# Block sums of the up weights made by accumulating transfers

## The chip, the cores and the metric

The kernel runs on one core of a Trainium2 chip. A core has a matrix engine (TensorE, PE in the profile, with its weight loads as PEld), a vector engine (VectorE, DVE), a scalar engine (ScalarE, ACT), GpSimd (POOL), a queue processor that issues transfers (SyncE, SP) and 16 DMA engines that all transfers share. The engines run side by side and wait for one another by semaphores; each works through its own instructions in order. The metric is the device time of one execution in microseconds.

## The reference

One layer of a diffusion backbone over 1024 tokens of width 1024. A token mixer with two kinds of attention is followed by a layer norm and a ConvFFN, which is the part that matters here:

```python
def _conv_ffn(h, w_up, conv_w, conv_b, w_down):
    u = h @ w_up                                # (1024 x 1024) @ (1024 x 5632)
    half = CONV_WIDTH // 2                      # width 3, one filter per channel
    u = lax.conv_general_dilated(u, conv_w[:, None, :], window_strides=(1,), padding=((half, half),),
                                 dimension_numbers=("NWC", "WIO", "NWC"),
                                 feature_group_count=u.shape[-1]) + conv_b
    gate, val = jnp.split(u, 2, axis=-1)
    return (jax.nn.silu(gate) * val) @ w_down
...
        x = _layer_norm(DEEPNORM_ALPHA * x + gate1 * y, ln1_g[l], ln1_b[l])
        h = x * (1.0 + scale2) + shift2
        y = _conv_ffn(h, w_up[l], conv_w[l], conv_b[l], w_down[l])
```

All numbers are fp32. `w_up` has 22 blocks of 128 gate columns and 22 of 128 value columns.

## The kernel before

**Precision.** An fp32 matrix is split into a high part (rounded to the matrix engine's format, on ACT) and a low part (the rest: a subtraction on DVE or GpSimd). A product then takes three matmuls, high x high, high x low, low x high (`split`, `mm3`). So every weight tile costs a cast and a subtraction before PE can use it.

**Stages.** Attention runs to about 765 us, then the branch merge, the output projection and the first layer norm to about 960 us, the up stage to 1363 us, the down stage and the second layer norm to the end.

**The up stage.** Tiles j = 0, 1, 2 are computed plainly (`up_conv`). Tiles 3 to 21 (`up_tile`) use a Strassen-Winograd scheme with seven products in place of eight. The 2 x 2 blocks on the weights' side are: A11, A12 the gate columns of tile j for the lower and upper half of the 1024 input channels, A21, A22 the value columns likewise. The activations' blocks B11, B21, B12, B22 are the two halves of the channels by the two halves of the tokens. Sums of blocks are needed on both sides:

- weights, per tile: S1 = A21 + A22, S2 = S1 - A11, S3 = A11 - A21, S4 = A12 - S2 (`wsums`, four additions of 128 x 512 on GpSimd into the tiles s12 and s34);
- activations, once: T1 to T4 in the tiles t13 and t24 (`build`, four steps k, each split into T13h, T13l, T24h, T24l).

Each product is 4 x 3 = 12 matmuls of 512 columns, so a tile is 84 matmuls. They accumulate in four PSUM banks a, b, c, d, and the results are combined on the way out: `pe` and `ve` are scratch tiles, `ug` and `uv` the gate and value rows before the convolution, `tg` and `tv` after it. The convolution of one half is an ACT activation and two DVE steps (`conv3`), then Silu on ACT, a product on DVE (`gated`) and a store of 512 KB to DRAM (`gd`).

**Loads and splits.** `wload(j)` loads the gate and value blocks of a tile as two transfers of 512 KB into a ring of three buffers (`raw`, tiles ru0 and ru1). `pairs` splits a weight or a sum into a tile of one of two rings (`w` and `wd`, four buffers each); the high parts are cast on ACT, and the table `UE` says which engine makes the low part: DVE for five of the seven, GpSimd for S4 and A22. The sums live in a ring of four buffers, `m`, which `build` uses for t13 and t24 before it. Three of the value rows' additions out of PSUM are on DVE and one is on GpSimd (the last argument of `add`).

**What sets the order.** PE's order is that of the code (a manual schedule). On ACT, DVE, GpSimd and SP a scheduler orders the instructions when the kernel is built. In the steady state it casts and splits the weights of tile j + 1 during tile j.

The convolution's weights lie in `cvw` and are loaded near the end of attention, when `cvt`, the tile they share with attention's row statistics, comes free.

Of the kernel before, what the change touches and what calls it, by code (L numbers as in the profile page):

```python
# [22 lines left out]
NF = FF // P  # L23
# [4 lines left out]
HALF = 512  # L28
# [24 lines left out]
OTB = 2  # L53
PSU = 6, 7, 2, 3, 4, 5, 0, 1
PSO = 4, 5, 0, 1, 7, 6, 2, 3
UE = "vector", "vector", "vector", "vector", "vector", "gpsimd", "gpsimd"
LN2_P = 1, 2, 2
GAP = 1
LN1_S = slice(0, 512), slice(512, 768), slice(768, 1024)
# [6 lines left out]
def layer_kernel(  # L66
# [6 lines left out]
    nc = tc.nc  # L73
    PSUM = bass.MemoryType.PSUM

    def split(src, hi, lo, hi_eng, lo_eng):
        if hi_eng is nc.scalar:
            nc.scalar.copy(hi, src)  # L78
# [4 lines left out]
        lo_eng.tensor_tensor(out=lo, in0=src, in1=hi.bitcast(F32), op=ALU.subtract)  # L83
# [24 lines left out]
    cvw, cvb = cvt[:, 0:6 * NF].rearrange("p (a b) -> p a b", b=3), cvt[:, 6 * NF:8 * NF]  # L108
# [115 lines left out]
    for k in range(KT):  # L224
# [5 lines left out]
        for t in range(NT):  # L230
            s = slice(t * P, (t + 1) * P)
# [437 lines left out]
    for n, (gi, k) in enumerate(order):  # L669
# [160 lines left out]
    av_issue(True)  # L830
    nc.sync.dma_start(cvw, conv)
# [208 lines left out]
    def sub(e, o, a, b, op=ALU.subtract):  # L1040
        e.tensor_tensor(out=o, in0=a, in1=b, op=op)
# [30 lines left out]
    def build(k):  # L1072
        (b11, b21), (b12, b22) = [[z[:, a] for a in (0, 1)] for z in (zt_[k, 0], tp["v", k])]
        st = {}

        def parts(a, e):
            for p in "hl":
                tp[a + p, k] = ht(f"T{a}{p}_{k}", (P, 2, HALF), R32)
            nc.scalar.copy(tp[a + "h", k], st[a])
            sub(e, tp[a + "l", k], st[a], tp[a + "h", k].bitcast(F32))  # L1080

        def s1():
            st["13"] = t = tm(f"t13_{k}").rearrange("p (a q) -> p a q", a=2)
            sub(nc.vector, t[:, 1], b12, b11)
            sub(nc.gpsimd, t[:, 0], b22, b12)

        def s2():
            st["24"] = t = tm(f"t24_{k}").rearrange("p (a q) -> p a q", a=2)
            sub(nc.vector, t[:, 1], b22, st["13"][:, 1])
            sub(nc.gpsimd if k % 2 else nc.vector, t[:, 0], b21, t[:, 1])  # L1090
            hput(f"z{k}_0", f"v{k}")

        return [s1, s2, lambda: parts("13", nc.vector), lambda: parts("24", nc.vector)]
# [158 lines left out]
        ps3.tile([P, HALF], F32, tag=f"u{n}", name=f"u{n}")  # L1252

    def wload(j):
        wraw[j] = [post.tile([P, 8, P], F32, tag="raw", name=f"ru{gv}_{j}", bufs=3) for gv in (0, 1)]
        for gv in (0, 1):
            nc.sync.dma_start(wraw[j][gv], w_up[2 * j + gv])
        (a11, a12), (_, a22) = [[r[:, 4 * n:4 * n + 4].rearrange("p a b -> p (a b)") for n in (0, 1)]
                                for r in wraw[j]]
        wsrc[j, "A11"], wsrc[j, "A12"], wsrc[j, "A22"] = a11, a12, a22  # L1260

    def wsums(j, mk):
        (a11, a12), (a21, a22) = [[r[:, 4 * n:4 * n + 4].rearrange("p a b -> p (a b)") for n in (0, 1)]
                                  for r in wraw.pop(j)]
# [4 lines left out]
        wsrc.update({(j, "S1"): s12[:, 0], (j, "S2"): s12[:, 1], (j, "S3"): s34[:, 0], (j, "S4"): s34[:, 1]})  # L1269
# [17 lines left out]
    def add(o, p, q, e=nc.vector):  # L1287
        e.tensor_tensor(out=o, in0=p, in1=q, op=ALU.add)  # L1288

    lohalf, hihalf = slice(0, HALF), slice(HALF, T)  # L1290

    def up_tile(j):
        a, b, c, d = (bank(f"{n}{j}") for n in "abcd")
        pe, ve = ht(f"pe{j}", (P, 2, HALF)), ht(f"ve{j}", (P, 2, HALF))
        ug, uv, tg, tv = (ht(f"{n}{j}") for n in ("ug", "uv", "tg", "tv"))
        prod(j, "A11", a, True, True)
        nc.scalar.copy(pe[:, 0], a)
# [9 lines left out]
        nc.scalar.copy(pe[:, 1], c)  # L1307
# [5 lines left out]
        add(ug[:, hihalf], c, ve[:, 0])  # L1313
        conv3(tg, ug, j)
        nc.scalar.activation(tg, tg, AF.Silu)
        pairs(j + 1, "S2", "S3", "S1")
        prod(j, "A22", d, False, True)
        add(uv[:, lohalf], d, ve[:, 0])
        conv3(tv, uv, NF + j)
        gated(j, tg, tv)  # L1320
        hput(*[f"{n}{j}" for n in ("pe", "ug", "ve", "uv", "tg", "tv")])

    wload(NCL)
    wsums(NCL, tm)
# [46 lines left out]
    for j in range(NF):  # L1371
        w, g = wdl.pop(0)
# [221 lines left out]
```

## Time and profile before

| | us |
|---|---|
| median of 3 runs | 1631.38 (1628.08 to 1635.48) |
| the profiled execution | 1630.69 |
| its span, on which all times below stand | 1628.9 |
| tiles 3 to 21 of the up stage | 994.7 to 1363.6 |

In a row of a timeline stand the start, the duration, the engine, the line, the operation, output and inputs by the program's names (without numbers), the shape, the count, and in square brackets the time that the engine stood idle before and what it waited for. In a group of instructions stand the shape and count, then busy time and the mean of one in ns, then the idle time before them and its causes. In a table by windows stand, for each stretch, the busy time of each engine with its count, the granted clock of PE, the mean busy share of the DMA engines and what they moved. `s` in the profile stands for s12 and s34, `wA` for the split weights and `wS` for the split sums, `t` for t13 and t24, `ru` for ru0 and ru1. SPq is SP's queue.

### The profile page before, as it was taken

Reading aid. Unit: us, or ns where it says so; the run is one execution under the profiler, and the core shown is the slowest. Engines: PE = TensorE matmul, PEld = TensorE weight load, DVE = VectorE, ACT = ScalarE, POOL = GpSimd, SP = SyncE. Lnnn points to the kernel's source line nnn. Section 1 sums busy time; section 2 is a strip of 40 time slices with the busy share of each in tenths; the row PEclk is TensorE's granted clock in tenths of the full one; section 3 lists DMA queues with packets and bytes.
Section 4 is the critical chain, followed back from the end, with each engine's and each line's share of the span. In section 5 each row is a group of like instructions: output and inputs, shape, how many; then the busy total and the mean of one; then the engine's idle time right before and its main releaser. Section 6 shows DMA issues by size and latency. Waiting matters only on the chain.

```text
span 1628.9 us, 22394 instructions
## 1 busy us (share of the span) xinstructions
PE 1563.2 (96%) x7944; PEld 1303.5 (80%) x7944; DVE 1173.0 (72%) x1692; ACT 813.5 (50%) x1468; POOL 844.0 (52%) x756
## 2 busy tenths in 40 slices
PE   6999999999999999999999989999999999999996
PEld 5878788888877887777788877888888888888896
DVE  7797646548887677887756695899999996335445
ACT  5322222358887667777223563444444444443343
POOL 0573302526665555655225353666776663337785
PEclk9999999999999999999999999999999999999998
DMA  9695662322230111011440211222222228653453
GB/s 379 211 318 179 213 206 84 117 74 60 61 100 21 46 33 46 24 27 61 158 155 32 99 65 65 78 78 78 78 80 89 88 97 301 218 189 96 149 164 110
DMA packets 86801, 192.52 MB, mean 118 GB/s; under 512 B 11040, under 2 KB 25888, under 8 KB 86688
## 3 DMA queue, kind: packets, MB, share of 16 engines
q1 hardware_dynamic: 81648, 181.63, 33.7%
q10 hardware_dynamic: 5040, 9.46, 1.6%
q8 instruction: 62, 1.02, 0.2%
q14 instruction: 51, 0.42, 0.1%
HBM read 154.28 MB, written 28.38 MB: 112 GB/s over the span
## 4 chain that ended last, share of the span: by engine, by line
PE 80%; DVE 7%; ACT 4%; DMA 3%; issue 3%; POOL 2%; SPq 0%; ACTq 0%; DVEq 0%; POOLq 0%
PE ptr L524 5%; PE g L86 3%; PE g L87 3%; PE g L88 3%; PE b L88 3%; PE b L87 3%; PE b L86 3%; PE ya L88 2%; PE ya L87 2%; PE ya L86 2%; PE av L545 2%; PE av L546 2%; PE d L86 2%; PE d L87 2%; PE yl L86 2%
## 5 line engine op out<-in xcount | busy, mean ns | idle before, releaser
L534 DVE TENSOR_TENSOR ptl<-ptr,pth 128x512 fp32r<-128x512 f32 x188 | 125.0, 685 | 22.5 <-ACT pth L533 19.8
L533 ACT CAST pth<-ptr 128x512 fp32r<-128x512 f32 x188 | 106.7, 587 | 63.7 <-PE ptr L524 37.6
L524 PE MATMUL ptr<-ident,p 128*128 128x128 f32 x816 | 127.2, 278 | 7.0 <-DVE ptl L534 5.1
L420 ACT ACTIVATE p<-p,nm 128x1024 f32<-128x1024 f32 (+2 forms) x128 | 125.3, 981 | 5.6 <-DVE p L453 4.6
L524 PEld LDWEIGHTS ptr<-ident,p 128*128 128x128 f32 x816 | 94.0, 140 | 36.7 <-DVE ptl L534 13.1
L545 PE MATMUL av<-pth,VT 128*128 128x512 f32 x236 | 104.4, 442 | 0.7 <-ACT avs L551 0.5
L83 POOL TENSOR_TENSOR wlg<-wg,whg 128x512 fp32r<-128x512 f32 x32 | 44.8, 1407 | 112.9 <-ACT whg L78 112.9
L86 PE MATMUL g<-hh,whg 128*128 128x512 f32 x256 | 99.9, 390 | 0.0
L88 PE MATMUL g<-hh,wlg 128*128 128x512 f32 x256 | 99.7, 390 | 0.0
L87 PE MATMUL g<-hl,whg 128*128 128x512 f32 x256 | 99.6, 389 | 0.0
L546 PE MATMUL av<-ptl,VT 128*128 128x512 f32 x236 | 97.6, 414 | 2.0 <-POOL ptl L83 1.8
L453 DVE TENSOR_SCALAR_CACHE_REDUCE p<-s,cvt,nmc 128x1024 f32<-128x1024 f32 x64 | 84.3, 1339 | 13.4 <-PE s L409 13.2
L83 POOL TENSOR_TENSOR lwf<-rwf,hwf 128x1024 fp32r<-128x1024 f32 (+1 forms) x36 | 82.3, 2302 | 12.4 <-ACT hwf L78 12.4
L86 PE MATMUL yl<-gr,hwf 128*128 128x256 f32 (+1 forms) x264 | 85.4, 323 | 0.0
L88 PE MATMUL yl<-gr,lwf 128*128 128x256 f32 (+1 forms) x264 | 84.2, 319 | 0.1
L87 PE MATMUL yl<-gr,hwf 128*128 128x256 f32 (+1 forms) x264 | 84.0, 318 | 0.0
L408 PE MATMUL s<-KL,q 128*128 128x512 f32 (+2 forms) x192 | 76.1, 396 | 5.1 <-ACT p_x L420 4.3
L83 POOL TENSOR_TENSOR lwd<-rwd,hwd 128x1024 fp32r<-128x1024 f32 x16 | 38.8, 2423 | 75.0 <-ACT hwd L78 60.6
L80 POOL TENSOR_SCALAR pth<-prw 128x512 fp32r<-128x512 f32 x48 | 30.1, 628 | 90.3 <-ACT prw L530 64.8
L182 DVE CUSTOM_DVE_ANT_0 wml<-wml,sc,bmc 128x1024 f32<-128x1024 f32 x32 | 44.6, 1406 | 40.1 <-DMA wml<-in_wmodT_dram 39.8
L409 PE MATMUL s<-KL,q 128*128 128x512 f32 (+2 forms) x192 | 71.5, 373 | 0.0
L1288 POOL TENSOR_TENSOR uv<-ve,pe 128x512 f32<-128x512 f32 x19 | 29.9, 1573 | 77.2 <-DVE ve L1288 38.1
(387 smaller groups left out, 5295.3 us busy)
## 6 DMA issues: line engine op xcount, KB each, us to landing
wml<-in_wmodT_dram SPq DMA_DIRECT2D x48, 512.0 KB
ru<-in_w_up_dram SPq DMA_DIRECT2D x38, 512.0 KB
rwf<-in_w_dnf_dram SPq DMA_DIRECT2D x24, 512.0 KB
rg<-gd SPq DMA_DIRECT2D x44, 256.0 KB
rwd<-in_w_dn_dram SPq DMA_DIRECT2D x22, 512.0 KB
gd<-tg SPq DMA_DIRECT2D x19, 512.0 KB
wm<-in_wmodT_dram SPq DMA_DIRECT2D x16, 512.0 KB
wg<-in_w_g_dram SPq DMA_DIRECT2D x32, 256.0 KB
```

What stands on the lines that cost most here:

```text
L83: lo_eng.tensor_tensor(out=lo, in0=src, in1=hi.bitcast(F32), op=ALU.subtract)
L86: nc.tensor.matmul(ps, a[0], b[0], start=start, stop=False, skip_group_check=resumed)
L87: nc.tensor.matmul(ps, a[0], b[1], start=False, stop=False, skip_group_check=resumed)
L88: nc.tensor.matmul(ps, a[1], b[0], start=False, stop=stop, skip_group_check=resumed)
L408: nc.tensor.matmul(o, self.q[0][:, hs], ks, start=True, stop=False)
L420: nc.scalar.activation(p, s, AF.Exp, bias=nm[:, h:h + 1], scale=scale, accum_out=sm[:, h:h + 1])
L453: nc.vector.tensor_scalar(out=p, in0=o, scalar1=self.qscale(nqs)[:, hs] if self.br else -1.0, scalar2=self.other[:, hs], op0=ALU.mult, op1 ...
L524: nc.tensor.transpose(tr[:, h * P:(h + 1) * P], self.pslice(h, n), ident)
L533: nc.scalar.copy(hi, tr)
L534: nc.vector.tensor_tensor(out=lo, in0=tr, in1=hi.bitcast(F32), op=ALU.subtract)
L545: nc.tensor.matmul(self.av, v, hi, start=first, stop=False)
L546: nc.tensor.matmul(self.av, v, lo, start=False, stop=self.left == 0)
```

## The change

1. The sums of the weights' blocks are no longer computed on GpSimd. `wsums` makes two tiles, s32 (S3 and S2) and s41 (S4 and S1). SP loads A21 into both halves of both; then GpSimd issues five transfers that add to what lies there: A11 to both halves of s32 (512 KB), A22 to both halves of s41 (512 KB), A22 to S2 (256 KB), A11 to S4 and A12 to S4 (256 KB each). An addition to bytes that an earlier transfer writes waits for it.
2. An accumulating transfer only adds. So the value rows of the scheme are computed with the sign turned: the subtractions of `build` change their order, S2's product is subtracted from `pe`, and the convolution's weights of the value columns of tiles 3 to 21 are multiplied by -1 once, by a new DVE instruction behind their load.
3. `wload` loads only the upper half of the value block (A22, 256 KB).
4. The low parts of S4 and A22 and the fifth addition of the value rows go from GpSimd to DVE. GpSimd has no vector work left in these tiles.
5. S1's product changes places with S3's; it is added straight from PSUM into `uv`, so one copy out of PSUM on ACT (128 x 512) is gone. `pe` and `ve` become the halves of one tile, `pv`.

GpSimd's instructions for one tile in the middle of the stage, before:

```order
L1041 TENSOR_TENSOR s12_9_11238<-ru1_9_11235 128x512
L1041 TENSOR_TENSOR s34_9_11239<-ru0_9_11234,ru1_9_11235 128x512
L1041 TENSOR_TENSOR s12_9_11238<-s12_9_11238,ru0_9_11234 128x512
L83 TENSOR_TENSOR wA22_8_11231<-ru1_8_11093,wA22_8_11231 128x512
L1041 TENSOR_TENSOR s34_9_11239<-ru0_9_11234,s12_9_11238 128x512
L1288 TENSOR_TENSOR uv8_11183<-ve8_11181,pe8_11180 128x512
L83 TENSOR_TENSOR wS4_9_11370<-s34_9_11239,wS4_9_11370 128x512
```

and for two tiles, after (the number behind a name is the tile's, the last one the buffer's):

```order
L1272 DMA s32_8_11103<-in_w_up_dram 128x2x512
L1272 DMA s32_8_11103<-in_w_up_dram 128x512
L1272 DMA s41_8_11104<-in_w_up_dram 128x2x512
L1272 DMA s41_8_11104<-in_w_up_dram 128x512 x2
L1272 DMA s32_9_11246<-in_w_up_dram 128x2x512
L1272 DMA s32_9_11246<-in_w_up_dram 128x512
L1272 DMA s41_9_11247<-in_w_up_dram 128x2x512
L1272 DMA s41_9_11247<-in_w_up_dram 128x512 x2
```

Seven vector instructions per tile become five issues of transfers; the second on s32 and the last two on s41 each wait for the one ahead on the same tile. The prediction calls them A1, A2 (s32) and A3, A4, A5 (s41).

SP's instructions in the middle of the stage, before (ru0 and ru1 are the gate and value loads, gd the stores):

```order
L1184 DMA gd5_84<-tg5_10758 128x1024
L1257 DMA ru1_8_11093<-in_w_up_dram 128x1024
L1257 DMA ru0_9_11234<-in_w_up_dram 128x1024
L1184 DMA gd6_85<-tg6_10900 128x1024
L1257 DMA ru1_9_11235<-in_w_up_dram 128x1024
L1257 DMA ru0_10_11376<-in_w_up_dram 128x1024
```

and after:

```order
L1184 DMA gd5_84<-tg5_10763 128x1024
L1269 DMA s32_9_11246<-in_w_up_dram 128x2x512
L1258 DMA ru1_8_11100<-in_w_up_dram 128x512
L1270 DMA s41_9_11247<-in_w_up_dram 128x2x512
L1257 DMA ru0_9_11242<-in_w_up_dram 128x1024
L1184 DMA gd6_85<-tg6_10906 128x1024
```

Two loads per tile are added; those into s32 and s41 stand a tile ahead of the value load, since their buffers come free when the sums of two tiles before are split.

ACT's casts where the stage begins (tile 3; c0_2 and c1_2 are the gate and value rows of tile 2 in their convolution, T24h the last operands of `build`), before:

```order
L1176 ACTIVATE c1_1_10262<-u1_1_10199,cvt_70 128x1024
L78 CAST wS2_3_10457<-s12_3_10448 128x512
L78 CAST wS1_3_10463<-s12_3_10448 128x512
L78 CAST wS3_3_10460<-s34_3_10449 128x512
L1079 CAST T24h_2_10398<-t24_2_10370 128x1024
L78 CAST wA12_3_10515<-ru0_3_10444 128x512
L1176 ACTIVATE c0_2_10338<-u0_2_10275,cvt_70 128x1024
L78 CAST wS4_3_10518<-s34_3_10449 128x512
L1217 ACTIVATE c0_2_10338<-c0_2_10338 128x1024
L78 CAST wA22_3_10521<-ru1_3_10445 128x512
L1176 ACTIVATE c1_2_10411<-u1_2_10348,cvt_70 128x1024
```

and after:

```order
L1176 ACTIVATE c1_1_10263<-u1_1_10200,cvt_70 128x1024
L1079 CAST T24h_2_10399<-t24_2_10371 128x1024
L77 CAST wS1_3_10464<-s41_3_10450 128x512
L77 CAST wS2_3_10461<-s32_3_10449 128x512
L77 CAST wS3_3_10467<-s32_3_10449 128x512
L77 CAST wA12_3_10518<-ru0_3_10445 128x512
L1176 ACTIVATE c0_2_10339<-u0_2_10276,cvt_70 128x1024
L77 CAST wS4_3_10521<-s41_3_10450 128x512
L1217 ACTIVATE c0_2_10339<-c0_2_10339 128x1024
L77 CAST wA22_3_10524<-ru1_3_10446 128x512
L1176 ACTIVATE c1_2_10412<-u1_2_10349,cvt_70 128x1024
```

The cast of T24h moves ahead of the sums' casts, and S1 ahead of S2; the cast of S4 keeps its place ahead of the last convolution's ACTIVATE.

The diff, cut to its core:

```diff
@@ near the end of attention
     nc.sync.dma_start(cvw, conv)
     nc.sync.dma_start(cvb, convb)
+    nc.vector.tensor_scalar(out=cvw[:, NF + NCL:], in0=cvw[:, NF + NCL:], scalar1=-1.0, scalar2=None, op0=ALU.mult)
@@ build
-            sub(nc.vector, t[:, 1], b12, b11)
+            sub(nc.vector, t[:, 1], b11, b12)
...
-            sub(nc.vector, t[:, 1], b22, st["13"][:, 1])
-            sub(nc.gpsimd if k % 2 else nc.vector, t[:, 0], b21, t[:, 1])
+            sub(nc.vector, t[:, 1], b22, st["13"][:, 1], ALU.add)
+            sub(nc.gpsimd if k % 2 else nc.vector, t[:, 0], t[:, 1], b21)
@@ wload
-            nc.sync.dma_start(wraw[j][gv], w_up[2 * j + gv])
...
+        nc.sync.dma_start(g, w_up[2 * j])
+        nc.sync.dma_start(v, w_up[2 * j + 1][:, 4:8])
@@ wsums
-        s12, s34 = (mk(f"s{a}_{j}").rearrange("p (a b) -> p a b", a=2) for a in ("12", "34"))
-        for o, a, b, op in ((s12[:, 0], a21, a22, ALU.add), (s12[:, 1], s12[:, 0], a11, ALU.subtract),
-                            (s34[:, 0], a11, a21, ALU.subtract), (s34[:, 1], a12, s12[:, 1], ALU.subtract)):
-            sub(nc.gpsimd, o, a, b, op)
+        lo, hi = (mk(f"s{a}_{j}").rearrange("p (n a b) -> p n a b", n=2, b=P) for a in ("32", "41"))
+        (a11, a12), (a21, a22) = [[w_up[2 * j + n][:, 4 * m:4 * m + 4] for m in (0, 1)] for n in (0, 1)]
+
+        def twice(a):
+            return a.unsqueeze(1).to_broadcast([P, 2, 4, P])
+
+        nc.sync.dma_start(lo, twice(a21))
+        nc.sync.dma_start(hi, twice(a21))
+        for o, a in ((lo, twice(a11)), (hi, twice(a22)), (lo[:, 1], a22), (hi[:, 0], a11), (hi[:, 0], a12)):
+            nc.gpsimd.dma_start(o, a, accum_op=ALU.add)
...
@@ pairs
-            split(wsrc.pop((j, n)), t[:, 0], t[:, 1], nc.scalar, getattr(nc, UE[list(prods).index(n)]))
+            split(wsrc.pop((j, n)), t[:, 0], t[:, 1], nc.scalar, nc.vector)
@@ up_tile
         prod(j, "S2", b, True, True)
-        add(ve[:, 0], b, pe[:, 0])
-        prod(j, "S3", d, True, True)
-        add(ve[:, 1], d, ve[:, 0])
+        sub(nc.vector, ve, pe, b)
+        prod(j, "S1", c, True, True)
+        add(uv[:, hihalf], c, ve)
...
-        prod(j, "S1", c, True, True)
-        nc.scalar.copy(pe[:, 1], c)
-        add(uv[:, hihalf], ve[:, 1], pe[:, 1], nc.gpsimd)
+        prod(j, "S3", d, True, True)
+        add(uv[:, hihalf], d, uv[:, hihalf])
```

More of the change, by code (lines that the diff above doesn't have):

```diff
@@ L55 @@
 PSO = 4, 5, 0, 1, 7, 6, 2, 3
-UE = "vector", "vector", "vector", "vector", "vector", "gpsimd", "gpsimd"
 LN2_P = 1, 2, 2
@@ L1168, in wdn_load @@
         return w, g
-    prods = {"A11": "B11", "S2": "T2", "S3": "T3", "S1": "T1", "A12": "B21", "S4": "B22", "A22": "T4"}
+    prods = {"A11": "B11", "S2": "T2", "S1": "T1", "S3": "T3", "A12": "B21", "S4": "B22", "A22": "T4"}
     wsrc, wtile, wraw = {}, {}, {}
@@ L1254, in wload @@
     def wload(j):
[L1255 to L1260, printed above, removed]
-    def wsums(j, mk):
-        (a11, a12), (a21, a22) = [[r[:, 4 * n:4 * n + 4].rearrange("p a b -> p (a b)") for n in (0, 1)]
-                                  for r in wraw.pop(j)]
-        s12, s34 = (mk(f"s{a}_{j}").rearrange("p (a b) -> p a b", a=2) for a in ("12", "34"))
-        for o, a, b, op in ((s12[:, 0], a21, a22, ALU.add), (s12[:, 1], s12[:, 0], a11, ALU.subtract),
-                            (s34[:, 0], a11, a21, ALU.subtract), (s34[:, 1], a12, s12[:, 1], ALU.subtract)):
-            sub(nc.gpsimd, o, a, b, op)
-        wsrc.update({(j, "S1"): s12[:, 0], (j, "S2"): s12[:, 1], (j, "S3"): s34[:, 0], (j, "S4"): s34[:, 1]})
+        g = post.tile([P, 8, P], F32, tag="raw", name=f"ru0_{j}", bufs=3)
+        v = post.tile([P, 8, P], F32, tag="raw", name=f"ru1_{j}", bufs=3)[:, 4:8]
+        nc.sync.dma_start(g, w_up[2 * j])
+        nc.sync.dma_start(v, w_up[2 * j + 1][:, 4:8])
+        for n, t in (("A11", g[:, 0:4]), ("A12", g[:, 4:8]), ("A22", v)):
+            wsrc[j, n] = t.rearrange("p a b -> p (a b)")
+    def wsums(j, mk):
+        lo, hi = (mk(f"s{a}_{j}").rearrange("p (n a b) -> p n a b", n=2, b=P) for a in ("32", "41"))
[6 more added lines that the diff above has]
+            nc.gpsimd.dma_start(o, a, accum_op=ALU.add)
+        for n, t in (("S3", lo[:, 0]), ("S2", lo[:, 1]), ("S4", hi[:, 0]), ("S1", hi[:, 1])):
+            wsrc[j, n] = t.rearrange("p a b -> p (a b)")
     def pairs(j, *names):
@@ L1285, in prod, with add @@
             tick(HALF / 0.8)
-    def add(o, p, q, e=nc.vector):
-        e.tensor_tensor(out=o, in0=p, in1=q, op=ALU.add)
+    def add(o, p, q):
+        nc.vector.tensor_tensor(out=o, in0=p, in1=q, op=ALU.add)
     lohalf, hihalf = slice(0, HALF), slice(HALF, T)
@@ L1293, in up_tile @@
         a, b, c, d = (bank(f"{n}{j}") for n in "abcd")
-        pe, ve = ht(f"pe{j}", (P, 2, HALF)), ht(f"ve{j}", (P, 2, HALF))
+        pv = ht(f"pv{j}", (P, 2, HALF))
+        pe, ve = pv[:, 0], pv[:, 1]
         ug, uv, tg, tv = (ht(f"{n}{j}") for n in ("ug", "uv", "tg", "tv"))
         prod(j, "A11", a, True, True)
-        nc.scalar.copy(pe[:, 0], a)
+        nc.scalar.copy(pe, a)
         prod(j, "S2", b, True, True)
-        add(ve[:, 0], b, pe[:, 0])
-        prod(j, "S3", d, True, True)
-        add(ve[:, 1], d, ve[:, 0])
+        sub(nc.vector, ve, pe, b)
+        prod(j, "S1", c, True, True)
+        add(uv[:, hihalf], c, ve)
         pairs(j, "A12", "S4", "A22")
@@ L1312, in up_tile @@
         prod(j, "S4", c, False, True)
-        add(ug[:, hihalf], c, ve[:, 0])
+        add(ug[:, hihalf], c, ve)
         conv3(tg, ug, j)
         nc.scalar.activation(tg, tg, AF.Silu)
-        pairs(j + 1, "S2", "S3", "S1")
+        pairs(j + 1, "S2", "S1", "S3")
         prod(j, "A22", d, False, True)
-        add(uv[:, lohalf], d, ve[:, 0])
+        add(uv[:, lohalf], d, ve)
         conv3(tv, uv, NF + j)
         gated(j, tg, tv)
-        hput(*[f"{n}{j}" for n in ("pe", "ug", "ve", "uv", "tg", "tv")])
+        hput(*[f"{n}{j}" for n in ("pv", "ug", "uv", "tg", "tv")])
     wload(NCL)
     wsums(NCL, tm)
-    pairs(NCL, "A11", "S2", "S3", "S1")
+    pairs(NCL, "A11", "S2", "S1", "S3")
     for j in range(NCL, NF):
```

## The prediction

> **What bounds the kernel now.** I read the page first, then the stage that the change rewrites: busy time by windows, the order of PE's instructions, the groups inside the stage, the chain where the stage begins.
>
> ```profile
> span 1628.9 us, 22394 instructions
> PE 1563.2 (96%) x7944; PEld 1303.5 (80%) x7944; DVE 1173.0 (72%) x1692; ACT 813.5 (50%) x1468; POOL 844.0 (52%) x756
> ```
>
> The profiled execution took 1630.69 us, 1.8 us more than its span and 0.7 us under the median of the three runs, 1631.38. The sum below is made against 1630.7. PE is the bound on average, so the question is where in the up stage (tiles 3 to 21) it is not.
>
> ```profile
> core 0: us, PE busy (x) PEld busy (x) DVE busy (x) ACT busy (x) POOL busy (x), PEclk, DMA share, GB/s
> 1000.00:1010.00 10.00, 7.54 (x19) 5.62 (x20) 4.61 (x7) 3.29 (x5) 0.00 (x0) 0.66 0.13 52
> 1060.00:1100.00 40.00, 40.00 (x178) 33.14 (x177) 36.95 (x30) 19.41 (x27) 27.39 (x16) 1.00 0.22 80
> 1300.00:1340.00 40.00, 40.00 (x176) 32.61 (x175) 37.18 (x31) 17.25 (x25) 26.84 (x14) 1.00 0.26 93
> 1360.00:1380.00 20.00, 20.00 (x90) 16.57 (x89) 14.54 (x14) 10.08 (x13) 5.39 (x3) 1.00 1.02 365
> 994.70:1363.56 368.86, 366.01 (x1597) 301.05 (x1596) 324.19 (x264) 173.83 (x248) 232.95 (x125) 0.99 0.26 92
> 1096.22 0.39 PE L86 MATMUL a<-B,wA 128*128 128x512 f32 x1
> 1115.26 0.39 PE L86 MATMUL a<-B,wA 128*128 128x512 f32 x1
> ```
>
> In the middle of the stage PE is busy in every microsecond at full clock. The last two rows are the first matmuls of two successive tiles: one tile takes 19.04 us for 84 matmuls, 0.227 us each. DVE is busy 37 of 40 us there and POOL 27, but PE hides both. The 19 tiles run from 994.70 to 1363.56 (where the next stage's first matmul stands): 368.86 us, against 19 x 19.04 = 361.8. So the whole stage holds only 7.1 us, 0.44% of the kernel, that are not matmuls at full pace. Most of this is at its start:
>
> ```profile
> 1001.96 0.75 PE L86 MATMUL b<-T24h,wS 128*128 128x512 f32 x1 [2.34 <-ACT T24h L1079]
> 1003.22 0.79 PE L87 MATMUL b<-T24l,wS 128*128 128x512 f32 x1 [0.51 <-DVE T24l L1041]
> 1004.66 0.63 PE L87 MATMUL d<-T13l,wS 128*128 128x512 f32 x1
> 1005.09 0.63 PE L88 MATMUL d<-T13h,wS 128*128 128x512 f32 x1
> ```
>
> PE waits 2.34 + 0.51 us for the last operand of the first S2 product, and then runs at a lower clock (0.66 in the window from 1000 to 1010; a matmul every 0.43 us until 1008.9, some 2.8 us more than at 0.227). That leaves 1.4 us of losses in all the other tiles.
>
> **The change, part by part.** A half per cent of this kernel is 8.2 us, about what a measurement can tell from no change. No gain inside the stage reaches it, since 7.1 us is all there is.
>
> *Work taken off POOL and given to DVE.* The groups between 1010 and 1340 us:
>
> ```profile
> L83 DVE TENSOR_TENSOR wA<-ru,wA 128x512 fp32r<-128x512 f32 x34 | 60.1, 1769 | 2.6 <-ACT wA L78 2.6
> L1177 DVE SCALAR_TENSOR_TENSOR tv<-uv,cvt,tv 128x1023 f32<-128x1023 f32 x17 | 39.2, 2307 | 0.0
> L1041 POOL TENSOR_TENSOR s<-ru,s 128x512 f32<-128x512 f32 x17 | 35.5, 2087 | 0.0
> L1288 POOL TENSOR_TENSOR uv<-ve,pe 128x512 f32<-128x512 f32 x17 | 27.0, 1588 | 74.2 <-DVE ve L1288 38.1 <-ACT pe L1307 16.1 <-PE c L88 6.7
> L1177 DVE SCALAR_TENSOR_TENSOR tg<-ug,cvt,tg 128x1023 f32<-128x1023 f32 x17 | 22.9, 1350 | 23.6 <-ACT tg L1176 23.6
> L1183 DVE TENSOR_TENSOR tg<-tg,tv 128x1024 f32<-128x1024 f32 x17 | 26.1, 1536 | 0.0
> L1288 DVE TENSOR_TENSOR uv<-d,ve 128x512 f32<-128x512 f32 x17 | 11.6, 683 | 0.0
> ```
>
> POOL loses per tile four sums, two splits and one add. DVE gains the two splits and the add, and ACT loses one copy out of PSUM. The same DVE operation costs 2307 ns where POOL works beside it and 1350 ns where it mostly does not, so with POOL silent DVE should need 12 operations of 512 columns at 0.68, four convolution steps at 1.3 and one product at about 1.2: 14.6 us of 19.04, against 17.6 now (36.95 of 40). Both are behind PE; what it can return is the 1.4 us. I take all of it: -1.4 us.
>
> *The accumulating transfers.* Per tile SP issues the gate rows (512 KB), half the value rows (256 KB, was 512) and two new loads of 512 KB; POOL issues five accumulating transfers, two of 512 KB (A1 on s32, A3 on s41) and three of 256 KB (A2 on s32; A4, A5 on s41). No such transfer is in the trace. The nearest rows are a plain one:
>
> ```profile
> 1113.10 11.47 SPq L1257 DMA_DIRECT2D ru<-in_w_up_dram  x2
> 1116.75 1.29 POOL L1041 TENSOR_TENSOR s<-ru 128x512 f32<-128x512 f32 x1 [2.56 <-DMA ru<-in_w_up_dram]
> ```
>
> 512 KB take 3.65 us from issue to use. By the window with share 1.02 at 365 GB/s they occupy the 16 DMA engines for 1.44 us, which leaves 2.2 us that do not grow with size. The low bound is a plain transfer: 3.65 and 2.9 us for 512 and 256 KB. An accumulation reads the tile as well as the source and then writes, so I price its engine time at two to three times the plain one: 5.1 and 3.65 us at twice, 6.5 and 4.4 at three times, the high bound. I take twice, since a copy already reads and writes and only one read is added. The Trainium skill ("Collectives: The Full Stack", on the bandwidth ceiling) says the same of reductions in the DMA engines: the addition is free, the second source read halves the rate (1.93 measured there). No run here shows it yet. By that rule the sum below is 1633.4, by the plain row 1630.5.
>
> ```profile
> 990.18 1.28 POOL L1041 TENSOR_TENSOR s<-ru,ru 128x512 f32<-128x512 f32 x1
> 1104.58 0.62 ACT L78 CAST wS<-s 128x512 fp32r<-128x512 f32 x1 [0.60 <-PE d L88]
> 1110.50 0.63 ACT L78 CAST wS<-s 128x512 fp32r<-128x512 f32 x1
> ```
>
> POOL works through its queue in order, and A2 waits for A1, A4 for A3, A5 for A4. Per tile that is A1 + A3 + A4 and two issues; I price an issue at 1.3 us, POOL's shortest sum (first row): 5.1 + 5.1 + 3.65 + 2.6 = 16.5 us. The plain loads and the store (2.25 MB, 6.5 us of engine time) share the engines; if four tenths meet an accumulation, 2.6 us are added: 19.1, equal to the tile. The queue has a lead. In the tile that began at 1096.22 the last two rows cast S1 (8.4 us into it) and S4 (14.3), both of the tile after it. The buffer of s41 comes free about 15 us into a tile with the split of S4 and serves the sums of two tiles on, whose S4 is cast 2 x 19.04 us after this one. A load and A3, A4, A5 take 3.65 + 12.4 = 16.1 of these 37 us. So about 21 us are in hand for 17 tiles, 1.2 us per tile, and the queue fails only above 20.2 us. Cost in the loop at twice the engine time: nothing.
>
> *The entry.* Here there is no lead, because the buffers of the first sums are those of the T operands' build:
>
> ```profile
> 971.03 1.21 DVE L1041 TENSOR_TENSOR T13l<-t,T13h 128x1024 fp32r<-128x1024 f32 x1
> 978.77 2.31 DVE L1183 TENSOR_TENSOR c<-c,c 128x1024 f32<-128x1024 f32 x1
> 981.16 1.05 ACT L1079 CAST T24h<-t 128x1024 fp32r<-128x1024 f32 x1 [0.52 <-DVE c L1183]
> 983.31 1.21 DVE L1041 TENSOR_TENSOR T24l<-t,T24h 128x1024 fp32r<-128x1024 f32 x1
> 988.25 1.06 ACT L1217 ACTIVATE c<-c 128x1024 f32<-128x1024 f32 x1 [2.22 <-DVE c L1179]
> 994.67 0.62 ACT L78 CAST wA<-ru 128x512 fp32r<-128x512 f32 x1 [5.36 <-PE u L87]
> 995.20 1.20 ACT L1176 ACTIVATE c<-u,cvt 128x1024 f32<-128x1024 f32 x1
> 996.43 1.28 DVE L1177 SCALAR_TENSOR_TENSOR c<-u,cvt,c 128x1023 f32<-128x1023 f32 x1 [8.28 <-ACT c L1176]
> 1000.86 1.04 ACT L1079 CAST T24h<-t 128x1024 fp32r<-128x1024 f32 x1 [3.95 <-DVE c L1183]
> ```
>
> The loads of s32 and s41 wait for the two T splits (971.03 and 983.31). With DVE uncontended and ACT's T24h moved ahead of the S casts, the second ends near 981. Then s41 lands at 984.65, A3 at 989.75, A4 at 993.4, A5 at 997.05. ACT's cast of S4 waits for A5, and behind it in ACT's queue stand a Silu (1.06), the cast of A22 (0.62) and the last convolution's ACTIVATE, which now ends at 996.4 and would end at 997.05 + 0.62 + 1.06 + 0.62 + 1.2 = 1000.55. The chain from there to PE's wait is as before, so PE waits 4.1 us longer. Bounds: 1.2 us at plain price, 7.0 at three times. I take 4.1, as for the price of the transfers.
>
> *The sign turn.* One small operation on DVE, which waits for a load:
>
> ```profile
> 758.49 0.36 SPq L831 DMA_DIRECT2D cvt<-in_conv_dram  x1
> 760.90 1.87 DVE L534 TENSOR_TENSOR ptl<-ptr,pth 128x512 fp32r<-128x512 f32 x3
> 764.54 0.69 DVE L534 TENSOR_TENSOR ptl<-ptr,pth 128x512 fp32r<-128x512 f32 x1 [1.77 <-ACT pth L533]
> ```
>
> It stands between these two DVE rows, in a gap of 1.77 us, over 4 us after the load was issued: 0. The turned subtractions in the build and the swap of S1 and S3 have the old sizes and count: 0.
>
> **Sum:** 1630.7 + 4.1 - 1.4 = 1633.4 us.
>
> **The rivals.** *The transfers become the bound* (the other side). If accumulation costs three times the engine time, POOL's queue needs 6.5 + 6.5 + 4.4 + 2.6 + 2.6 = 22.6 us per tile, 3.6 over the tile; 17 tiles less the 21 us in hand give 40, with the longer entry about 1675. It decides above 20.2 us, an engine time of about 2.3 times the plain one. For it: my own sum stands at 19.1, and nothing in the trace bounds the price from above. At 3.5 times it is about 1703.
>
> *DVE holds POOL's issues up.* POOL's own sums go from 1.28 us (row at 990.18, DVE idle) to 2.09 on average beside DVE (the group above). If five issues each lose 0.6 us, half a convolution step, the queue grows by 3 us: 3 x 17 - 21 = 30, about 1664. Against it: an issue reads no tile. The Trainium skill ("SBUF — State Buffer", who interferes with whom) names this trap for transfers issued by GpSimd, but only beside DVE copies and tensor-scalar operations, which the loop does not have; by that rule it does not happen.
>
> *The entry alone is much longer*: if the first three accumulations on s41 take 18 us in place of 12.4, the entry costs 9.7 us and more, about 1641.
>
> *Faster by over 0.5%* would need the whole 7.1 us and more from outside the stage.
>
> **How the numbers follow.** Forecast case 0.50 (its own range 1624 to 1639: all 7.1 us won, or the high entry), transfers as the bound 0.33, issues held up 0.06, long entry 0.08, over 0.5% faster 0.03. Slower is 0.47, same 0.50. The range goes from 1624, all stalls gone, to 1700, just under 3.5 times the engine time; I leave out 0.03 below and some 0.14 above.
>
> **What would show it.** DVE's operations of 512 columns near 0.68 us and the convolution steps near 1.3; PE at 40.00 of 40 in the middle of the stage; ACT's cast of S4 at the entry waiting for a POOL transfer until about 997, and PE's wait for T24h between 6 and 7 us. Wrong would be: PE waiting for wS in each tile, ACT waiting for transfers throughout, tiles of over 20 us.

## The result, and the profile after

The changed kernel takes 1680.97 us (median of 4 runs, 1680.18 to 1685.42) against 1632.02 us before: 1.0306 times the time, with an interval of 1.0276 to 1.0336. It is slower by 49 us. The profiled execution took 1680.18 us, 49.5 more than the one before.

From the page of the kernel after (total, busy time of the engines; shares of the chain that ended last; the costliest groups on the sums):

```profile
span 1678.4 us, 22640 instructions
PE 1581.8 (94%) x7944; PEld 1313.6 (78%) x7944; DVE 1107.6 (66%) x1750; ACT 803.0 (48%) x1449; POOL 701.5 (42%) x718
...
PE 50%; issue 18%; DVE 11%; DMA 9%; POOL 7%; ACT 5%; SPq 0%; ACTq 0%; POOLq 0%; DVEq 0%
...
L1272 POOL DMA_DIRECT2D s<-in_w_up_dram x95 | 97.3, 1139 | 315.4 <-DMA s<-in_w_up_dram 303.9
L82 DVE TENSOR_TENSOR wS<-s,wS 128x512 fp32r<-128x512 f32 x76 | 52.3, 690 | 130.9 <-ACT wS L77 129.9
L77 ACT CAST wS<-s 128x512 fp32r<-128x512 f32 x76 | 45.6, 620 | 184.3 <-DMA s<-in_w_up_dram 174.6
```

POOL's 95 issues (five for each of 19 tiles) wait 303.9 us for accumulating transfers, and ACT's casts of the sums wait 174.6 us for the same. Before, POOL's sums waited for plain loads and ACT's casts for POOL's sums, and both far less (850 to 1350 us; total, times, longest):

```profile
POOL s L1041 <- DMA ru<-in_w_up_dram: 45.0, 18, 2.8
ACT wS L78 <- POOL s L1041: 35.8, 18, 3.5
```

**Where the 49 us are.** First matmuls of A11's product in the kernel after, of tiles 3, 4, 8 and 21, then the first rows of tiles 4 and 21 before (tile 3 began at 994.70 there):

```profile
999.59 0.39 PE L85 MATMUL a<-B,wA 128*128 128x512 f32 x1
1029.13 0.39 PE L85 MATMUL a<-B,wA 128*128 128x512 f32 x1
1105.79 0.39 PE L85 MATMUL a<-B,wA 128*128 128x512 f32 x1
1393.49 0.39 PE L85 MATMUL a<-B,wA 128*128 128x512 f32 x1
```

```profile
1020.06 0.39 PE L86 MATMUL a<-B,wA 128*128 128x512 f32 x1
1344.52 0.39 PE L86 MATMUL a<-B,wA 128*128 128x512 f32 x1
```

- Ahead of the stage 4.9 us (999.59 against 994.70). In the traces the rows are 1.9 us apart by 910 us and 3.4 by 957; from 780 to 800 us PE's granted clock was 0.88 and 0.95 where the execution before had 1.00. In the twelve traces of this case the stage starts anywhere between 994.5 and 1002.6, on average at 998.7 in the eight with transfers on POOL and at 998.3 in the four without. I do not count it as the change's. So some 44 us have their place in the stage; whether any of the other 5 belongs to the change, these runs do not tell.
- Tile 3: 29.54 us against 25.36, 4.2 more.
- Tiles 4 to 20: 364.36 us (1029.13 to 1393.49) against 324.46, 39.9 more. Tiles 4 to 7 still take about 19.04 each ((1105.79 - 1029.13) / 4 = 19.17); the 13 from tile 8 on take 22.13 on average.

Busy time by windows in the kernel after, of the start, of the tiles that still run at full pace, and of the slow ones:

```profile
1000.00:1010.00 10.00, 4.51 (x20) 3.39 (x19) 4.64 (x6) 3.70 (x5) 2.79 (x3) 0.97 1.07 229
1010.00:1020.00 10.00, 7.01 (x23) 5.37 (x24) 5.89 (x8) 3.39 (x5) 2.27 (x3) 0.69 1.05 268
1020.00:1060.00 40.00, 40.00 (x179) 33.11 (x178) 28.11 (x36) 18.16 (x25) 10.20 (x10) 1.00 0.84 201
1105.00:1345.00 240.00, 218.94 (x907) 176.73 (x906) 147.90 (x185) 92.92 (x132) 54.22 (x53) 0.95 0.83 189
```

In the last row PE is idle for 21 of 240 us and runs at 0.95 of its clock for the rest, so that 907 matmuls take the time of 1057 at 0.227 us. The DMA engines are busy 0.83 of the time: much more than before (0.22), and still not full. DVE, alone now, is far from its limit (148 of 240 us).

POOL's queue in the middle of the stage (each row an issue or two; in brackets the wait ahead of it). The rows with x1 are A4; x2 are A5 with the next tile's A1, and A2 with A3:

```profile
1111.75 2.13 POOL L1272 DMA_DIRECT2D s<-in_w_up_dram  x2 [7.15 <-DMA s<-in_w_up_dram]
1120.98 0.90 POOL L1272 DMA_DIRECT2D s<-in_w_up_dram  x1 [7.10 <-DMA s<-in_w_up_dram]
1125.24 2.09 POOL L1272 DMA_DIRECT2D s<-in_w_up_dram  x2 [3.36 <-DMA s<-in_w_up_dram]
1134.05 2.13 POOL L1272 DMA_DIRECT2D s<-in_w_up_dram  x2 [6.72 <-DMA s<-in_w_up_dram]
```

From A2 and A3 of one tile to those of the next pass 22.3 us, and all of it is POOL's own waits and issues: 7.10 us until A3 has landed, 3.36 until A4, 6.72 until A1, and five issues. Over ten tiles the means are 7.07 + 3.84 + 6.28 us of waits and 5.13 of issues, 22.3 us per tile; over 15 tiles (1043.57 to 1376.73) it is 22.2 us per tile, against PE's 19.04. How that reaches PE stands in the waits from 960 to 1420 us (total, times, longest):

```profile
POOL s L1272 <- DMA s<-in_w_up_dram: 303.9, 58, 8.2
ACT wS L77 <- DMA s<-in_w_up_dram: 174.6, 48, 8.6
DVE wS L82 <- ACT wS L77: 129.9, 39, 7.7
PEld c L85 <- DVE uv L1293: 30.1, 14, 3.6
PE c L85 <- DVE uv L1293: 24.2, 13, 3.2
```

ACT's cast of a sum waits for the transfer, DVE's split for the cast, and behind that split, in DVE's queue, stands an addition of value rows that reads a PSUM bank. PE waits for this addition at the first product into bank c, so its wait carries a name that has little to do with the cause.

### The profile page after: what moved, and what is told of

It is laid out like the page before. It is cut to its first block, busy times and chain, and to the rows that moved or that the text cites. A ratio compares the mean times of both kernels' runs of the same rounds, so it can differ in the third digit from the quotient of the medians.

```text
span 1678.4 us, 22640 instructions
## 1 busy us (share of the span) xinstructions
PE 1581.8 (94%) x7944; PEld 1313.6 (78%) x7944; DVE 1107.6 (66%) x1750; ACT 803.0 (48%) x1449; POOL 701.5 (42%) x718
## 4 chain that ended last, share of the span: by engine, by line
PE 50%; issue 18%; DVE 11%; DMA 9%; POOL 7%; ACT 5%; SPq 0%; ACTq 0%; POOLq 0%; DVEq 0%
DMA s<-in_w_up_dram 5%; PE ptr L523 5%; POOL s L1272 4%; PE ya L87 2%; PE ya L86 2%; PE ya L85 2%; PE av L544 2%; PE av L545 2%; PE g L85 2%; PE g L86 2%; PE g L87 2%; PE s L407 2%; DMA wml<-in_wmodT_dram 2%; PE s L408 2%; PE yl L85 2%
## 5 line engine op out<-in xcount | busy, mean ns | idle before, releaser
L1272 POOL DMA_DIRECT2D s<-in_w_up_dram x95 | 97.3, 1139 | 315.4 <-DMA s<-in_w_up_dram 303.9
L533 DVE TENSOR_TENSOR ptl<-ptr,pth 128x512 fp32r<-128x512 f32 x188 | 125.1, 685 | 22.3 <-ACT pth L532 19.7
L82 DVE TENSOR_TENSOR wS<-s,wS 128x512 fp32r<-128x512 f32 x76 | 52.3, 690 | 130.9 <-ACT wS L77 129.9
L77 ACT CAST wS<-s 128x512 fp32r<-128x512 f32 x76 | 45.6, 620 | 184.3 <-DMA s<-in_w_up_dram 174.6
L407 PE MATMUL s<-KL,q 128*128 128x512 f32 (+2 forms) x192 | 76.1, 396 | 5.1 <-ACT p_x L419 4.3
```

What stands on the lines that cost most here:

```text
L407: nc.tensor.matmul(o, self.q[0][:, hs], ks, start=True, stop=False)
L533: nc.vector.tensor_tensor(out=lo, in0=tr, in1=hi.bitcast(F32), op=ALU.subtract)
L1272: nc.gpsimd.dma_start(o, a, accum_op=ALU.add)
```

## The experiments

"Serial queue" is the theory that POOL's waits for A1, A3 and A4, one after the other, set the pace; its rivals are that the DMA engines are full, that the other parts of the change cost the time, and that it is the addition, the contention or POOL's way of issuing that makes a transfer long.

### Is it the transfers at all?

The four sums made by GpSimd's vector additions again, with the value blocks loaded whole for them; all else is as in the change. Here and below the diffs are cut to their core.

```diff
 def wsums(j, mk):
-        nc.sync.dma_start(lo, twice(a21))
-        nc.sync.dma_start(hi, twice(a21))
-        for o, a in ((lo, twice(a11)), (hi, twice(a22)), (lo[:, 1], a22), (hi[:, 0], a11), (hi[:, 0], a12)):
-            nc.gpsimd.dma_start(o, a, accum_op=ALU.add)
+        for o, a, b in ((hi[:, 1], a21, a22), (lo[:, 1], hi[:, 1], a11),
+                        (lo[:, 0], a11, a21), (hi[:, 0], a12, lo[:, 1])):
+            sub(nc.gpsimd, o, a, b, ALU.add)
```

> The four sums are GpSimd's vector operations again (S1 = A21 + A22, S2 = S1 + A11, S3 = A11 + A21, S4 = A12 + S2), with whole value blocks loaded; the sign turn, the new order of the products and the moves to DVE stay. If the transfers are all that cost: 1630 to 1636 us, PE full in the middle of the stage. DVE would be the bound if it needs over 19.04 us per tile: 14.6 us uncontended and about 3.2 more beside 8.4 us of GpSimd sums (before: 5.0 more beside 13.0 us) are 17.8, so not; if the sums hit it harder (all its 512-column operations at 1.77 us) it needs some 22 and the time is about 1680.

Measured 1630.56 us against 1631.97, a ratio of 0.9995 (0.9982 to 1.0007). Its window in the middle of the stage:

```profile
1060.00:1100.00 40.00, 40.00 (x179) 33.10 (x178) 34.65 (x36) 18.94 (x26) 16.64 (x10) 1.00 0.24 79
```

PE is full and DVE has room (34.65 of 40). The sign turn, the new order of the products and DVE's three further operations cost nothing that can be measured, and gain nothing that the time shows. The loss belongs to the transfers, and not to the rest of the change.

### What makes a transfer long?

Without the addition, the same five transfers only overwrite, and the sums are not formed:

```diff
-            nc.gpsimd.dma_start(o, a, accum_op=ALU.add)
+            nc.gpsimd.dma_start(o, a)
```

> The five transfers on POOL with the same bytes, places and waits, but each overwrites in place of adding (so S1 to S4 are not computed; the values are those of single blocks). If the addition is what makes them long: landing near the plain 3.65 and 2.9 us plus contention, so about 5 and 3.5 us, the queue 5 + 5 + 3.5 + 2.2 = 15.7 us per tile, no stalls of PE in the loop, about 1637 us. If any transfer that POOL issues is that slow: landing stays at 8.0 and 4.7 us, 1681 us.

Measured 1631.90 us, a ratio of 1.0003 (0.9984 to 1.0022); the profiled execution took 1639.12. DMA queues from 1105 to 1345 us (packets, MB, share of the 16 engines; then issues by size with the median us to landing), of this kernel and of the changed one; POOL's transfers are the software queue:

```profile
q0 software_dynamic: 6212, 21.57, 27.8%
...
s<-in_w_up_dram POOLq DMA_DIRECT2D x23, 512.0 KB, 5.5
...
s<-in_w_up_dram POOLq DMA_DIRECT2D x36, 256.0 KB, 3.4
```

```profile
q0 software_dynamic: 10577, 19.90, 50.3%
...
s<-in_w_up_dram POOLq DMA_DIRECT2D x21, 512.0 KB, 7.9
s<-in_w_up_dram POOLq DMA_DIRECT2D x32, 256.0 KB, 4.7
```

With the same places, order and waits the loop is hidden again. An accumulation took 0.503 x 240 / 19.90 = 6.07 us of the engines per MB, an overwriting transfer 0.278 x 240 / 21.57 = 3.09: a ratio of 1.96. Landing grows from 5.5 to 7.9 us and from 3.4 to 4.7. So it is the addition; that POOL issues the transfer is not enough. An issue is longer with it, too: 0.86 to 1.20 us against 0.54 to 0.71.

Contention was to show in two kernels. One loads the gate and upper value rows for tile 3 only:

```diff
 def wload(j):
-        nc.sync.dma_start(g, w_up[2 * j])
-        nc.sync.dma_start(v, w_up[2 * j + 1][:, 4:8])
+        if j == NCL:            # later tiles keep these rows
+            nc.sync.dma_start(g, w_up[2 * j])
+            nc.sync.dma_start(v, w_up[2 * j + 1][:, 4:8])
```

> The accumulating transfers as they are, but the gate and upper value rows (768 KB per tile, a third of the plain bytes) are loaded for tile 3 only, and all later tiles use those rows for A11, A12 and A22 (their own loads are left out; the sums still read the right blocks). If contention with the plain transfers is a part of the 8.0 and 4.7 us: about 2.6 of the 8.0 us by the sum of 2.2 fixed and 3.2 engine time, a third less of it gives 7.1 and 4.3, the queue falls from 22.4 to about 20.2 and the time to about 1652 us. If an accumulation takes as long by itself: 1681 us.

The other also loads A21 for two tiles only:

```diff
+        if j < NCL + 2:         # later tiles go on adding to the sums of j - 2
             nc.sync.dma_start(lo, twice(a21))
             nc.sync.dma_start(hi, twice(a21))
```

> The accumulating transfers nearly alone: as with fewer loads, and A21 too is loaded only for tiles 3 and 4; later tiles go on adding to these two sets of sums, so their sums are not the block sums. Of the loop's plain transfers only the store of 512 KB is left; the order on POOL is the serial one. If an accumulation costs twice a plain transfer's engine time and the rest was contention, 512 and 256 KB land in 5.1 and 3.65 us, the queue needs 16.5 us per tile and the loop is hidden, about 1635 us. If the length is the accumulation's own, landing stays at 7.7 and 4.3 us, and the queue at about 20 to 22 us with the time at 1650 to 1681.

Measured 1665.76 us (1.0197, 1.0166 to 1.0228) and 1646.29 (1.0088, 1.0067 to 1.0109). Landing in the second:

```profile
s<-in_w_up_dram POOLq DMA_DIRECT2D x24, 512.0 KB, 7.2
s<-in_w_up_dram POOLq DMA_DIRECT2D x35, 256.0 KB, 3.8
```

and its issues on POOL (x1 is A4, then A5 with the next A1, then A2 with A3):

```profile
1103.21 0.90 POOL L1281 DMA_DIRECT2D s<-in_w_up_dram  x1 [6.67 <-DMA s<-in_w_up_dram]
1107.15 2.09 POOL L1281 DMA_DIRECT2D s<-in_w_up_dram  x2 [3.04 <-DMA s<-in_w_up_dram]
1114.59 2.13 POOL L1281 DMA_DIRECT2D s<-in_w_up_dram  x2 [5.34 <-DMA s<-in_w_up_dram]
1123.15 0.90 POOL L1281 DMA_DIRECT2D s<-in_w_up_dram  x1 [6.44 <-DMA s<-in_w_up_dram]
```

Almost alone, the transfers still land in 7.2 and 3.8 us, and POOL's queue takes 20.3 us per tile (mean of 13, with waits of 6.55, 3.38 and 5.29 us for A3, A4 and A1). So contention is about 1.9 of the 22.2 us. With a third of the plain bytes gone it was 21.6, less of a fall than I expected, and the time 14 us above my figure; the profiled execution of that kernel (1674.39 us) was the slowest of its four, so 21.6 may be a little high. In the second kernel PE's excess is in its first tiles (31.28 and 23.23 us; all later ones 19.04): in tile 3 an addition of value rows comes late behind a cast that waits 9.0 us for a transfer, and the sums of tile 5 wait for the splits of tile 3 in place. These 16 us and what the queue has in hand (14 us, below) can cover the 1.3 us by which it is longer than a tile, so the loop is hidden although the transfers are not short.

### Is it the order of the waits?

The changed kernel's transfers, bytes and additions, in another order on POOL. The code lists them as A1, A3, A2, A4, A5; the scheduler had put A2 ahead of A3, and a manual schedule keeps the order of the code:

```diff
-            for o, a in ((lo, twice(a11)), (hi, twice(a22)), (lo[:, 1], a22), (hi[:, 0], a11), (hi[:, 0], a12)):
-                nc.gpsimd.dma_start(o, a, accum_op=ALU.add)
+        with tc.manual_schedule(engines={mybir.EngineType.Pool}):     # A1, A3, A2, A4, A5 as written
+            for o, a in ((lo, twice(a11)), (hi, twice(a22)), (lo[:, 1], a22), (hi[:, 0], a11), (hi[:, 0], a12)):
+                nc.gpsimd.dma_start(o, a, accum_op=ALU.add)
```

> The same transfers, but POOL issues A1, A3, A2, A4, A5 in this order, so that each wait for an accumulation has another one in flight beside it. Serial queue (POOL's period of 22.4 us per tile is the sum of the waits for A1, A3 and A4, one after the other, while the 16 DMA engines are busy 0.82 of the time): the waits overlap, the queue needs 16 to 18 us per tile, at the limit of the engines' own work (0.82 x 22.1 = 18.1 us), below the tile's 19.04; about 1640 us (1635 to 1648), POOL's waits no longer end in PE's. Engines bound by the bytes: the order changes nothing, 1681 +- 4 us with tiles of 22.1 us.

Measured 1638.92 us, a ratio of 1.0040 (1.0022 to 1.0059), as expected of a serial queue. Its window and its issues on POOL (x3 is A5 and the next tile's A1 and A3):

```profile
1105.00:1290.00 185.00, 185.00 (x818) 153.24 (x817) 132.46 (x165) 84.64 (x117) 49.09 (x48) 1.00 0.88 213
```

```profile
1108.35 3.33 POOL L1273 DMA_DIRECT2D s<-in_w_up_dram  x3 [5.67 <-DMA s<-in_w_up_dram]
1117.15 0.90 POOL L1273 DMA_DIRECT2D s<-in_w_up_dram  x1 [5.48 <-DMA s<-in_w_up_dram]
1120.55 0.86 POOL L1273 DMA_DIRECT2D s<-in_w_up_dram  x1 [2.50 <-DMA s<-in_w_up_dram]
1127.14 3.33 POOL L1273 DMA_DIRECT2D s<-in_w_up_dram  x3 [5.73 <-DMA s<-in_w_up_dram]
```

PE is full for 185 us. The order alone takes away 42 of the 49 us, with not a byte less. That the DMA engines are full was therefore not what held the changed kernel at 22.2 us. It is close, though: the interleaved queue runs at 19.4 us per tile ((1264.04 - 1050.51) / 11) with the engines busy 0.88, and has no room to spare. The 16 to 18 us that I expected of it were too low.

Then the two transfers that I had counted as free. A2 and A5, with a quarter of their bytes:

```diff
-            (lo[:, 1], a22), (hi[:, 0], a11), (hi[:, 0], a12)):
+            (lo[:, 1, 0:1], a22[:, 0:1]), (hi[:, 0], a11), (hi[:, 0, 0:1], a12[:, 0:1])):
```

> The order and all waits of the changed kernel, but A2 and A5 carry only the first 128 of their 512 columns (64 KB in place of 256; so three quarters of S2 lack A22 and of S4 lack A12). In the changed kernel POOL issues A2 right ahead of A3, and A5 right ahead of the next tile's A1, so each is in flight beside a transfer that POOL then waits for. If their bytes are what made A1 and A3 longer than the 5.1 us predicted (256 KB at twice the plain engine time are 1.44 us), the queue of 22.2 us per tile loses 2 x 1.1 us, A1 and A3 land near 6.9 us in place of 8.0, the excess over the tile is 1.1 us and its sum over 17 tiles (18) stays under the 21 us in hand: about 1640 us (1636 to 1648). If A1 and A3 are that long by themselves: landing 8.0 us, 1675 to 1681 us.

Measured 1651.47 us, a ratio of 1.0106 (1.0085 to 1.0127). Landing:

```profile
s<-in_w_up_dram POOLq DMA_DIRECT2D x24, 512.0 KB, 6.9
...
s<-in_w_up_dram POOLq DMA_DIRECT2D x12, 256.0 KB, 4.0
```

The 512 KB land in 6.9 us, as expected, and the queue takes 20.3 us per tile (mean of 13), 1.9 less where I had worked out 2.2. This returns 30 of the 49 us. The time is 11 us above my figure, since the lead of the queue is shorter than the 21 us that I gave it: 17 tiles with 1.3 us of excess each are 22 us, of which PE lost 14.3 in tiles 4 to 20, so about 8 were in hand.

### What is left: the start of the stage

In the interleaved kernel PE waits 8.41 + 0.46 us in tile 3. With the sums of that tile alone made by vector additions:

```diff
 def wsums(j, mk):
...
+        if j == NCL:
...
+            for o, x, y in ((s1, b21, b22), (s2, s1, b11), (s3, b11, b21), (s4, b12, s2)):
+                sub(nc.gpsimd, o, x, y, ALU.add)
+            return
```

> The interleaved order, and the sums of tile 3 alone made by GpSimd's vector additions (its value block loaded whole); tiles 4 to 21 by transfers. If what is left of the change's cost (1638.9 against 1632.0) is the entry, where PE waits 8.41 + 0.46 us for T24h and T24l: that wait falls to about 2.9 us and the time to about 1633 us. If it is spread over the loop or comes from other work: 1637 to 1639 us.

Measured 1634.32 us, a ratio of 1.0014 (1.0000 to 1.0028): tile 3 takes 24.37 us in place of 31.49. Most of what the interleaved order had left (0.40%, now 0.14%) was the entry.

That wait of PE is in the kernel before too. In tile 3 alone, the products that do not need T24 go first, once in the kernel with the sums by vector additions, and once in the kernel before (there S3 stands ahead of S1):

```diff
-        prod(j, "S2", b, True, True)            # tile 3: A11, S2, S1, S3
+        prod(j, "S1", c, True, True)            # tile 3: A11, S1, S3, S2
+        prod(j, "S3", d, True, True)
+        prod(j, "S2", b, True, True)
```

> The vector sums as in e2_vector_sums, and in tile 3 alone the products in the order A11, S1, S3, S2, so that the first product that needs T24 stands 5.4 us later. If the 2.34 us that PE waits there, and the lower clock behind this gap, are what tile 3 costs over the others (24.05 against 19.04 us): about 1626 us (1624 to 1629). If the clock goes down without the gap too: about 1628. If the wait comes back at another operand: 1630.6.

> The kernel before with the same late S2 in tile 3 (A11, S3, S1, S2): tile 3 takes 25.36 us there against 19.04. If the gap is the cause: about 1626 us, as in the run with vector sums. If not: 1632 us.

Measured 1627.39 us (0.9968, 0.9956 to 0.9980) and 1628.84 us (0.9973, 0.9958 to 0.9988). Tile 3 takes 19.04 us in both. The start of the stage with vector sums and late S2:

```profile
1000.00:1010.00 10.00, 10.00 (x46) 8.27 (x45) 7.50 (x9) 5.34 (x8) 0.00 (x0) 1.00 0.30 105
1010.00:1020.00 10.00, 10.00 (x46) 8.29 (x45) 6.54 (x9) 4.13 (x6) 3.57 (x3) 1.00 0.25 72
```

No gap and no low clock, so the gap was what made tile 3 long. Both are faster than either kernel of this case, by 0.3%, though 1.4 and 2.8 us above the 1626 that I expected; which of the two is better, these runs do not tell. The last one joins the interleaved order, the vector sums of tile 3 and the late S2:

> The interleaved order, the sums of tile 3 by vector additions, and S2 late in tile 3: the transfers with all that the runs found against them taken away. If nothing else of them costs: as with vector sums and late S2, about 1628 us (1626 to 1630). If their load on the DMA engines delays the start of the down stage (a tile of 19.43 us near the end in the run with the first sums by vector, 0.4 us, and 1634.3 against 1630.6 us): 1630 to 1632 us. No reason for less than 1626.

Measured 1636.67 us, a ratio of 1.0017 (1.0006 to 1.0028), no better than without the late S2 and 8 us over what I expected. Tile 3 takes 19.04 us here, but tile 7, tiles 9 to 12 and the last but one stall again (up to 22.79 us), some 9 us in sum. Its queue on POOL takes 19.7 us per tile ((1281.37 - 1045.20) / 12), 0.64 more than PE's 19.04: over 17 tiles 11 us, of which PE lost 9, so only about 2 were in hand. It seems that the shorter start leaves the queue less lead. Why this queue is slower than that of the other two interleaved kernels is not settled. In all three interleaved kernels the queue is slower than PE (19.4, 19.3 and 19.7 us per tile), so transfers with their order mended still give nothing that vector additions do not give.

## Why the prediction was right or wrong

The time lies inside the range, but by a rival: the forecast case (hidden, 1633.4 us) did not come true, and "the transfers become the bound" did, with 1681 us where it gave about 1675. The step that failed is the queue's sum per tile, 19.1 us; measured 22.2. Of the signs of being wrong, ACT's waits for transfers and tiles of over 20 us appeared; PE's wait carries another name than wS, as shown above.

- **The sum of the queue: failed.** I wrote "A1 + A3 + A4 and two issues" and gave A2 and A5 no time beyond their issue, because POOL does not wait for A2 before A3, nor for A5 before the next A1. But POOL issues each right ahead of the transfer that it then waits for, and both share the 16 engines. At my own price 256 KB are 1.44 us of engine time; 2 x 1.44 would have brought 19.1 to 22.0 us, above the 20.2 from which I had the queue fail. The run with small A2 and A5 shows it: three quarters of their bytes are 1.9 us of the queue. The rest of the 3.1 us is only known in part: from the issue of A4, which nothing of POOL's accompanies, to POOL's next issue pass 0.90 + 3.38 us even when almost alone, where I had 3.65, and 512 KB take 3.2 us of engine time (6.07 us per MB) where I had 2.9.
- **Twice the engine time: right.** It was 1.96 times the plain one of the same queue. The Trainium skill ("Collectives: The Full Stack", on the bandwidth ceiling) gives 1.93 for a second source read; this case's trace agrees with the figure. The rival had the engine time at three times, and its size came out (22.6 us per tile, 40 us) by luck, for another cause. The price was right and the sum of the queue was not.
- **Contention, 2.6 us: near**, about 1.9 us (22.2 against 20.3 almost alone).
- **21 us in hand: too much.** The excess is 17 x (22.2 - 19.04) = 54 us, and PE lost 39.9 in tiles 4 to 20, so about 14 were in hand. It seems that the fault is this: I had counted from when a buffer comes free to its use two tiles later, as if the queue began with that distance complete.
- **The entry, +4.1 us: right in its place, and in its size partly by luck.** Tile 3 costs 4.2 us more. ACT's row of the S4 cast, then the chain to PE, in the kernel after:

```profile
1003.76 0.62 ACT L77 CAST wS<-s 128x512 fp32r<-128x512 f32 x1 [6.16 <-DMA s<-in_w_up_dram]
...
1005.76 1.20 ACT L1176 ACTIVATE c<-u,cvt 128x1024 f32<-128x1024 f32 x1
...
1011.43 1.04 ACT L1079 CAST T24h<-t 128x1024 fp32r<-128x1024 f32 x1 [3.97 <-DVE c L1183]
```

```profile
1012.53 0.79 PE L85 MATMUL b<-T24h,wS 128*128 128x512 f32 x1 [8.01 <-ACT T24h L1079]
1013.78 0.79 PE L86 MATMUL b<-T24l,wS 128*128 128x512 f32 x1 [0.47 <-DVE T24l L1041]
```

  The chain is the one described, through A5, the cast of S4 and the last ACTIVATE. PE's wait is 8.48 us where I forecast 6 to 7; A5 too is in flight beside the next A1, which can account for the difference. Part of the low clock fell into this longer gap (0.50 from 1010 to 1012, while PE was idle), so that less of it was left for the matmuls, and this makes up for the wait.
- **DVE alone, -1.4 us: the durations were right, the gain is smaller.** DVE's splits take 0.69 us (forecast 0.68) and its convolution steps about 1.28 (1.3). Without the addition, where POOL is as silent, tiles 4 to 20 take 323.68 us against 324.46 before: 0.8 us, too little for the times to show. They take the same with vector sums, beside which DVE is not alone, so it is not shown that the faster DVE is what returns it.
- **DVE holding up POOL's issues (0.06): did not happen.** POOL's issues last 0.86 to 1.20 us in the middle of the loop, under the 1.3 that I took. The Trainium skill's rule ("SBUF — State Buffer", who interferes with whom) that this needs operations which the loop does not have agrees with it.
- **The sign turn, 0: right**, by the run with vector sums, which has it.

## What to carry to other kernels

When transfers are ordered on one queue, add up the time between two waits with every byte in flight in it, those that nobody waits for included. An engine that issues transfers which depend on one another is a serial resource: look for its period, not only for its busy share or that of the DMA engines. Before bytes are saved, try the order, so that each wait has another transfer to cover it; here that was worth 42 of 49 us. And a wait of the bound engine at the start of a stage can sometimes be filled by taking first the work whose operands are there.

## What was not expected of the hardware

- An accumulating transfer lands later than its own engine time. Almost alone, 512 KB (with 256 KB of another transfer beside them) land in 7.2 us and 256 KB in 3.8, although at 6.07 us per MB their own engine time is only 3.2 and 1.6. An estimate from the numbers of this case comes near: with the 2.2 us that the prediction found beside the engine time of a plain transfer, and 1.6 for the neighbour of the 512 KB, it gives 7.0 and 3.8. The packets are half as large as without the addition: 19.90 MB in 10577 (1.88 KB each) against 21.57 MB in 6212 (3.47 KB). Whether the smaller packets or the second source read named above make the rate was not separated.
- Transfers issued together are not independent: with A2 and A5 at a quarter, their neighbours land 1.0 us sooner (7.9 to 6.9). The Trainium skill gives a reason ("DMA: Bandwidth & Descriptors", on issuing engines that are not separate DMA queues): all transfers run interleaved on the same 16 engines. The trace agrees.
- A gap of PE of 2.34 + 0.51 us was followed by some 7 us at a low clock in the kernel before (0.66 on average from 1000 to 1010, 0.51 already from 1002 to 1004, a matmul every 0.43 us until 1008.9). With the gap filled the clock stays at 1.00, and tile 3 falls from 25.36 to 19.04 us, 6.3 us for 2.85 of waiting. The Trainium skill ("TensorE: Matmul & The Clock Gate", on the HAM clock gate) puts the drop after an idle window of about 3.4 us; here the first wait, 2.34 us, was enough, and the measurement decides.
